# Two tiles of a feed-forward projection without Strassen, token blocks made once, and a new order of the products

## The chip, the cores and the metric

The kernel runs on one core of a Trainium2 chip. A core has five engines with queues of their own: TensorE (PE, matmuls into PSUM), VectorE (DVE), ScalarE (ACT), GpSimd (POOL) and SyncE (SP, which issues DMAs here). The metric is the device time of one execution in microseconds, lower is better.

## The reference, cut to what matters

One layer of a transformer trunk for 512 latent and 128 context tokens of 1024 features. The change concerns its second half, from the output projection of the attention part to the first feed-forward projection:

```python
x += gate1 * (merged @ w_out)                       # 640 x 1024
h = rms_norm(x, norm2_w) * (1 + scale2) + shift2
a, up = split(h @ w_ffn_in)                         # 1024 -> 2 x 2816
a = dwconv3(a)                                      # along the tokens, latent and context apart
x += gate2 * ((silu(a) * up) @ w_ffn_out)           # 2816 -> 1024
y = rms_norm(x, final_norm_w)
```

## The kernel before, in words

Every float32 matrix is split into a high and a low part, `hi` and `lo` (a cast on ScalarE and a subtraction, usually on VectorE), and each product of 128 x 128 weights with 320 tokens is made of hi*hi, hi*lo and lo*hi. The 640 tokens are two halves of 320 (`HALF`), the 1024 features two halves of four blocks. So one block product, called a product here, is 4 x 3 = 12 matmuls.

The first feed-forward projection runs over 22 tiles of 128 columns. In a tile the column block of `a` (raw weights `raw_fa`) and that of `up` (`raw_fu`) against the two token halves would be eight products. The kernel uses Strassen's scheme in Winograd's form with seven: `product(i, p)` for p = 1, 2, 5, 6, 3, 7, 4. It needs sums of weight blocks (`sums`, four operations of 128 x 512 on POOL per tile) and differences of token blocks. Products 1, 2, 5 and 3 read `h2` (whose tiles print as `mg`), products 6, 7 and 4 read `hx`, the blocks that are sums. Two accumulators, `pfNA` and `pfNC` of tile N, are one PSUM pair, and `pb` takes product 2. Behind them `copy`, `add2`, `add3` and `add7` bring the parts together (`av`, `c`), `conv` makes one ScalarE and four VectorE operations into `cv`, `silu` and the multiplications (`glu2`, `glu1`) end in the split tile `g` (`glo` its low part).

The tiles are in three groups of 8, 7 and 7 (`GROUPS`). After a group the second projection (`out2_steps`) takes the group's tiles as its sum; weights come block by block through `fetch`. In group 0 it shares its time with the making of the second gate (`gate2`, matmuls `pb_g`). Within a group `cycle(i)` writes down the work of tile i, the rest of tile j = i - 1 and the weights of n = i + 1. `start` is the hand-written order of the first tiles. The order of each engine's instructions is the order in which the code is written (`Pin`), for PE, VectorE, ScalarE and POOL alike.

Ahead of `start`, `out_steps(t)` makes the output projection of token tile t (PSUM `pso`), the gated sum (`y`, `x`), the norm, and `modulate(t)` transposes the result (`pt`) and modulates it. For tokens of the second half `modulate` also makes, per token tile, the differences `e` and their splits, on VectorE and POOL. For the last token tile the first products of tiles 0, 1 and 2 are put ahead of its transposes.

## Time and profile before

| | |
|---|---|
| median of 3 runs (lowest to highest) | 1103.39 us (1103.24 to 1106.56) |
| the profiled execution | 1106.75 us |
| its span, first to last instruction | 1104.7 us |
| mean granted TensorE clock | 0.98 |
| busy: PE, DVE, ACT, POOL | 1046.0, 858.2, 549.2, 346.8 us |

The profiled execution is 0.3% above the median and 2 us longer than its span. Busy shares are means over stages that differ: the attention part, the 70 us around the start of the feed-forward part, and the long run of cycles after it.

### The profile page before, as it was taken

The numbers are of one execution on the slowest core, as the hardware profiler recorded it, in microseconds if no ns is written. First come the engines' busy times: TensorE is split into PE (matmuls) and PEld (weight loads), VectorE is DVE, ScalarE is ACT, GpSimd is POOL, SyncE is SP. The second block draws the span as 40 slices with busy tenths as digits, with TensorE's granted clock in tenths as the row PEclk, the third lists the DMA queues.
The fourth block names the chain that finished last, engine by engine and source line by source line (L and its number), as shares of the span: only waits on it lengthen the run. The fifth ranks groups of instructions, "written<-read, shape, count | busy, mean of one in ns | idle before, by whom it ended". The sixth has DMA issues, their size and how long they took to land. (4 is left out here: it accounts for less than half of the span.)

```text
span 1104.7 us, 16747 instructions
## 1 busy us (share of the span) xinstructions
PE 1046.0 (95%) x6535; PEld 974.3 (88%) x6535; DVE 858.2 (78%) x1197; ACT 549.2 (50%) x913; POOL 346.8 (31%) x279
## 2 busy tenths in 40 slices
PE   6988999999999999999999978899999999999997
PEld 4788899999999999999998768899789998899986
DVE  5968988988887577776763599899769984599847
ACT  8636667667665552222343554555344552255524
POOL 3544324323222630000000196344175320444202
PEclk9898999999999999999999989899999999999999
DMA  9830212112112135554562021324442232222412
GB/s 313 231 94 27 84 32 65 47 38 65 41 42 58 49 88 170 153 155 140 164 194 112 1 58 39 96 77 134 126 122 77 77 118 63 69 77 77 133 39 96
DMA packets 128481, 106.11 MB, mean 96 GB/s; under 512 B 4173, under 2 KB 110205, under 8 KB 128402
## 3 DMA queue, kind: packets, MB, share of 16 engines
q1 hardware_dynamic: 126450, 101.93, 30.6%
q0 software_dynamic: 1232, 1.80, 0.8%
q8 instruction: 51, 0.84, 0.3%
q10 hardware_dynamic: 720, 1.31, 0.3%
q14 instruction: 28, 0.23, 0.1%
HBM read 101.36 MB, written 3.67 MB: 95 GB/s over the span
## 5 line engine op out<-in xcount | busy, mean ns | idle before, releaser
L157 PE MATMUL ps_g<-hT,whi_g 128*128 128x320 f32 x512 | 96.7, 311 | 0.0
L150 DVE SCALAR_TENSOR_TENSOR cv<-av,vcol,cv 128x511 f32<-128x511 f32 (+1 forms) x84 | 85.5, 1038 | 7.7 <-ACT cv L150 6.4
L150 POOL TENSOR_TENSOR s<-raw_fu 128x512 f32<-128x512 f32 x20 | 30.2, 1509 | 165.4 <-DMA raw_fu<-in_w_ffn_in_dram 91.8
L157 PEld LDWEIGHTS ps_g<-hT,whi_g 128*128 128x128 f32 x512 | 80.2, 188 | 2.0 <-issue 1.5
L150 ACT CAST whi_f<-s 128x1024 fp32r<-128x1024 f32 x42 | 44.1, 1049 | 65.6 <-POOL s L150 54.5
L689 ACT ACTIVATE p<-s,nm 128x640 f32<-128x640 f32 (+1 forms) x80 | 56.5, 708 | 40.0 <-DVE nm L687 39.4
L157 PE MATMUL psv<-whi_v,hT 128*128 128x256 f32 x320 | 66.3, 287 | 0.0
L687 DVE TENSOR_REDUCE nm<-s 128x1 f32<-128x640 f32 (+1 forms) x80 | 56.6, 710 | 12.4 <-PE s L157 11.0
L150 DVE TENSOR_TENSOR wlo_f<-s,whi_f 128x1024 fp32r<-128x1024 f32 x42 | 54.7, 1302 | 8.8 <-ACT whi_f L150 8.8
L157 PE MATMUL ps_g<-hT,wlo_g 128*128 128x320 f32 x256 | 58.3, 309 | 0.0
L242 DVE SCALAR_TENSOR_TENSOR acc_g<-raw_g,silu,acc_g 128x512 f32<-128x512 f32 x48 | 40.9, 886 | 20.4 <-DMA raw_g<-in_w_ada_dram 18.9
L157 PE MATMUL s<-ks,qd 128*128 128x320 f32 x144 | 44.2, 318 | 10.3 <-DVE ks L598 7.1
L157 PEld LDWEIGHTS psv<-whi_v,hT 128*128 128x128 f32 x320 | 53.5, 193 | 0.3 <-ACT whi_v L126 0.3
L157 PE MATMUL psyb<-on,whi_pb 128*128 128x320 f32 x256 | 48.0, 309 | 0.0
L127 DVE TENSOR_TENSOR wlo_fo<-raw_fo,whi_fo 128x1024 fp32r<-128x1024 f32 (+1 forms) x24 | 28.3, 1179 | 23.6 <-ACT whi_fo L126 23.5
L157 PE MATMUL psv<-wlo_v,hT 128*128 128x256 f32 x160 | 45.6, 285 | 0.9 <-DVE wlo_v L127 0.9
L126 ACT CAST whi_fo<-raw_fo 128x1024 fp32r<-128x1024 f32 (+1 forms) x24 | 23.5, 978 | 39.6 <-PE acc101C L157 15.6
L157 PE MATMUL s<-ks,ql 128*128 128x320 f32 x144 | 43.0, 309 | 0.0
L157 PEld LDWEIGHTS ps_g<-hT,wlo_g 128*128 128x128 f32 x256 | 42.8, 188 | 0.0
L157 PE MATMUL psk<-hT,whi_k 128*128 128x320 f32 x224 | 42.6, 312 | 0.0
L157 PEld LDWEIGHTS psyb<-on,whi_pb 128*128 128x128 f32 x256 | 40.3, 188 | 0.5
L157 PE MATMUL pb<-mg,whi_f 128*128 128x320 f32 x176 | 40.6, 318 | 0.0
(1009 smaller groups left out, 3450.1 us busy)
## 6 DMA issues: line engine op xcount, KB each, us to landing
raw_fa<-in_w_ffn_in_dram SPq DMA_DIRECT2D x22, 512.0 KB, 4.5
raw_fu<-in_w_ffn_in_dram SPq DMA_DIRECT2D x20, 512.0 KB, 4.0
raw_fo<-in_w_ffn_out_dram SPq DMA_DIRECT2D x20, 512.0 KB, 4.8
raw_g<-in_w_in_dram SPq DMA_DIRECT2D x16, 512.0 KB, 4.6
raw_g<-in_w_ada_dram SPq DMA_DIRECT2D x16, 512.0 KB, 3.7
araw_sh<-in_w_ada_dram SPq DMA_DIRECT2D x8, 512.0 KB, 8.2
araw_sc<-in_w_ada_dram SPq DMA_DIRECT2D x8, 512.0 KB, 9.1
raw_v<-in_w_in_dram SPq DMA_DIRECT2D x8, 512.0 KB, 6.3
```

The lines of the kernel that those rows point to most:

```text
L126: nc.scalar.copy(hi[:, :n], rv)
L127: eng.tensor_tensor(lo[:, :n], rv, f(hi[:, :n]), ALU.subtract)
L150: pin(getattr(self.eng, op)(*args, **kw))
L157: pin(nc.tensor.matmul(out, s, m, start=start, stop=stop, skip_group_check=more))
L242: nc.vector.scalar_tensor_tensor(acc[:, c, :], raw[:, ki, :], w, acc[:, c, :], ALU.mult, ALU.add)
L687: nc.vector.tensor_reduce(nm[:, i:i + 1], s, AX.XY, ALU.max, negate=True)
L689: nc.scalar.activation(p.rearrange("p (b n) -> p b n", b=s.shape[1]), s, AF.Exp, bias=nm[:, i:i + 1], accum_out=z[:, i:i + 1])
```

## The change

Tiles 0 and 1 (`DIRECT`) are made as ordinary products, eight each: 1, 2, then Q, D, E, F, G and H, which read raw weights and `h2` alone. They need neither `sums` nor `hx`. Their parts are joined by `addD` and `glu_direct`.

`modulate` keeps all tokens in one tile, `hall`, and makes only the difference that `h2` itself needs, in place. The blocks of `hx` are made once, for all 320 tokens, by `blocks` and `block_lo` on VectorE behind the last token tile. POOL no longer takes part in this, nor in the low parts of the first weights. In the last token tile four products stand ahead of the transposes, and a high and a low part of tile 1's weights are put between its steps.

In a cycle the products go 1, 2, the last tile's 7, 5, 6, 3, the last tile's 4, where 4 stood ahead of 3; the splits follow in the order in which the products use them, each later than before. In group 0 `glo` follows four tiles late, so `cv` has three buffers.

The first weights of `out2_steps` are fetched in the last cycle of a group, `prepare` of the next group's first tile is in two parts, and the steps of the second gate go to the (block, token tile) pairs of `GATE2`. The operations of the gate's sums and of the fetched weights' splits now keep the written order too (not shown). Of `start` only the new lines are shown.

```diff
+    DIRECT = 2
+    R, S, W2, PS, PB, PD, AV, C22, CVS, GT = {}, {}, {}, {}, {}, {}, {}, {}, {}, {}
...
-        src = {1: lambda: R[i, 0], 2: lambda: S[i, 0], 3: lambda: S[i, 1], 4: lambda: R[i, 1][:, 4:, :]}[n]()
-        if n < 4:
+        src = {1: lambda: R[i, 0], 2: lambda: S[i, 0], 3: lambda: S[i, 1], 4: lambda: R[i, 1][:, 4:, :],
+               5: lambda: R[i, 1]}[n]()
+        if n != 4:
             w = [wpool.tile([P, KD, P], F32R, tag=t, name=f"{t}_f{n}_{i}") for t in ("whi", "wlo")]
...
+            for k0, ps in zip((0, 4), {1: ((1, "E"), (2, "F")), 2: ((5,), (6,)), 3: ((3,), (7,)),
+                                       5: (("Q", "G"), ("D", "H"))}[n]):
+                for p in ps:
+                    W2[i, p] = [x[:, k0:k0 + 4, :] for x in w]
...
+            elif p == "D":
+                PD[i] = psF.tile([P, 512], F32, tag="F", name=f"pd{i}")[:, :HALF]
+            out = {1: pa, 6: pa, 7: pa, 4: pa, 5: pc, 3: pc, 2: PB.get(i), "Q": pc, "D": PD.get(i),
+                   "E": pa, "F": pa, "G": pc, "H": pc}[p]
...
+    def addD(i):
+        dve.tensor_tensor(C22[i], C22[i], PD.pop(i), ALU.add)
+    def glu_direct(i):
+        dve.tensor_tensor(CVS[i][:, :HALF], CVS[i][:, :HALF], C22.pop(i), ALU.mult)
+        dve.tensor_tensor(CVS[i][:, HALF:], CVS[i][:, HALF:], PS.pop(i)[1][:, :HALF], ALU.mult)
...
+        cv = CVS[i] = pools["ffn"].tile([P, TOK], F32, tag="cv", name=f"cv{i}", bufs=3)
...
+        ghi(i)
+    def ghi(i):
...
+            if before:
+                before()
             half(1)
+            if between:
+                between()
...
-            h32 = h1[:, :, ts] if t < 2 else wo.tile([P, KD, P], F32, tag="h32", name=f"h32_{t}", bufs=1)
...
+            yield
+            c0, c1 = max(t * P, HALF), (t + 1) * P
+            if t * P < HALF:
+                cs = slice(t * P, min(c1, HALF))
+                split_to(h2[0][:, :, cs], h2[1][:, :, cs], hall[:, :, cs])
+            if c0 >= c1:
                 return
...
-            b12, b22 = h32[:, :4, lead:], h32[:, 4:, lead:]
-            e = wo.tile([P, 16, P], F32, tag="e", name=f"e{t}", bufs=1)
-            e1, e2, e3, e4 = (e[:, 4 * i:4 * i + 4, :n] for i in range(4))
-            dve.tensor_tensor(e1, b12, h1[:, :4, cs], ALU.subtract)
-            dve.tensor_tensor(e2, b22, e1, ALU.subtract)
-            split_to(h2[0][:, :4, c2], h2[1][:, :4, c2], e1)
+            c2, b12 = slice(c0, c1), hall[:, :4, c0:c1]
+            dve.tensor_tensor(b12, b12, hall[:, :4, c0 - HALF:c1 - HALF], ALU.subtract)
+            split_to(h2[0][:, :4, c2], h2[1][:, :4, c2], b12)
             yield
-            split_to(hx[0][:, :4, cs], hx[1][:, :4, cs], e2)
-            split_to(h2[0][:, 4:, c2], h2[1][:, 4:, c2], b22)
-            yield
-            pool.tensor_tensor(e3, b22, b12, ALU.subtract)
-            pool.tensor_tensor(e4, h1[:, 4:, cs], e2, ALU.subtract)
-            yield
-            split_to(hx[0][:, 4:, cs], hx[1][:, 4:, cs], e[:, 8:, :n], dve if t == NT - 1 else pool)
+            split_to(h2[0][:, 4:, c2], h2[1][:, 4:, c2], hall[:, 4:, c2])
+        def blocks(n):
+            b11, b21, e1, b22 = (hall[:, k:k + 4, c:c + HALF] for c in (0, HALF) for k in (0, 4))
+            e = EB[n] = spare[1][:, 2 * n:2 * n + 2, :].rearrange("p j n -> p (j n)").rearrange("p (k n) -> p k n", n=HALF)
+            x, y = ((b22, e1), (b21, EB.get(0)), (EB.get(0), b11))[n]
+            dve.tensor_tensor(e, x, y, ALU.subtract)
+            act.copy(hx[0][:, KB[n], :], e)
+        EB, KB = {}, (slice(0, 4), slice(8, 12), slice(4, 8))
+        def block_lo(n):
+            dve.tensor_tensor(hx[1][:, KB[n], :], EB[n], f(hx[0][:, KB[n], :]), ALU.subtract)
...
+            last = t == NT - 1
+            if last:
                 load(0, 0)
+                load(0, 1)
                 load(1, 0)
-                load(2, 0)
-            for n in out_steps(t, True):
+            for n in out_steps(t, True, last and (lambda: hi(1, 1)), last and (lambda: lo(1, 1))):
                 if n == (11, 9, 9)[t - 2]:
                     rest = modulate(t - 1)
-                    next(rest, None)
+                    next(rest)
                     next(rest, None)
                 elif n == (15, 13, 10)[t - 2]:
                     each(rest)
-                if t == NT - 1 and n in (1, 3):
-                    hi(n // 2, 1)
-                elif t == NT - 1 and n in (2, 4):
-                    lo(n // 4, 1, pool)
-                elif t == NT - 1 and n == 13:
-                    hi(2, 1)
+                if last and n == 1:
+                    hilo(0, 1)
+                elif last and n == 4:
+                    hilo(0, 5)
+                    load(1, 1)
         spare = [res.tile([P, 8, TOK], F32, tag=f"r{i}", name=f"spare{i}") for i in range(2)]
...
-        load(0, 1, room(0, 0))
-        load(1, 1, room(1, 0))
-        lo(2, 1, pool)
-        product(0, 1, 2)
-        product(1, 1)
-        copy1(0, spare[0][:, 7, :])
+        product(0, 1, 2, "Q", "D")
+        copy1(0, spare[0][:, 0, :])
         act.activation(warm2, eps, AF.Silu)
         add2(0)
-        sums(0, 0, room(0, 2))
         rest = modulate(NT - 1)
         next(rest)
-        product(2, 1)
-        product(1, 2)
-        hilo(0, 2)
-        sums(0, 1, room(1, 2))
+        hilo(1, 5)
+        copy5(0, spare[0][:, 2, :HALF])
+        addD(0)
+        load(2, 0)
+        load(2, 1)
+        product(1, 1, 2)
+        copy1(1, spare[0][:, 1, :])
         next(rest)
-        hilo(0, 3)
-        product(2, 2)
-        product(0, 5)
-        copy5(0, spare[1][:, 7, :HALF])
-        product(0, 6)
+        add2(1)
         each(rest)
+        product(1, "Q", "D")
+        copy5(1, spare[0][:, 3, :HALF])
+        addD(1)
+        for n in range(3):
+            blocks(n)
+        block_lo(0)
+        product(0, "E", "F")
+        copy6(0)
+        hilo(2, 1)
     actx.close()
...
-    def prepare(i):
-        load(i, 0)
-        load(i, 1)
+    def prepare(i, part):
+        if part == 0:
+            load(i, 0)
+            load(i, 1)
+            hilo(i, 1)
+            return
         sums(i, 0)
-        hilo(i, 1)
+        hilo(i, 2)
         sums(i, 1)
-        hilo(i, 2)
         hilo(i, 4)
         load(i + 1, 0)
-        hilo(i, 3)
         load(i + 1, 1)
-    def cycle(i, first, end):
...
+    def cycle(i, first, end, after):
         j, n = (i - 1 if i > first else None), (i + 1 if i < end else None)
...
         product(i, 1, 2)
         do(j, lambda j: product(j, 7))
         do(j, add3)
-        do(j - 1 if j is not None and j > first else None, glo)
+        copy1(i)
+        if i == DIRECT + 1:
+            lo(i, 3)
+        elif i == first:
+            hilo(i, 3)
+        if i - 4 >= GROUPS[0][0] and first == DIRECT:
+            glo(i - 4)
+        elif j is not None and j > first and first != DIRECT:
+            glo(j - 1)
         do(j, conv)
-        copy1(i)
         do(n, sums, 0)
-        do(n, hi, 2)
         add2(i)
         do(j, add7)
-        do(n, lo, 2)
+        product(i, 5)
+        copy5(i)
+        if n is None:
+            next(after)
+        do(n, hi, 1)
+        do(n, lo, 1)
         do(j, silu)
         do(j, glu2)
-        do(n, hi, 1)
-        product(i, 5)
+        do(n, hi, 2)
         do(n, sums, 1)
-        copy5(i)
-        do(n, lo, 1)
-        do(n, hi, 4)
-        do(n, lo, 4)
+        do(n, lo, 2)
+        if i == DIRECT + 1:
+            lo(i, 4)
         product(i, 6)
         if i + 2 <= end:
             load(i + 2, 0)
         copy6(i)
         do(n, hi, 3)
+        product(i, 3)
+        do(n, lo, 3)
         do(j, lambda j: product(j, 4))
+        do(n, hi, 4)
         do(j, glu1)
-        do(n, lo, 3)
-        product(i, 3)
+        do(n, lo, 4)
         if i + 2 <= end:
             load(i + 2, 1)
...
     def start():
...
+        sums(2, 0)
+        load(3, 0)
         conv(0)
+        product(0, "G", "H")
+        hilo(2, 2)
+        sums(2, 1)
+        load(3, 1)
+        product(1, "E", "F")
+        copy6(1)
         silu(0)
+        hi(2, 3)
+        glu_direct(0)
+        lo(2, 3)
+        product(1, "G", "H")
+        product(2, 1, 2)
         copy1(2)
+        sums(3, 0)
+        hi(3, 1)
         add2(2)
+        lo(3, 1)
+        hi(2, 4)
+        block_lo(2)
+        product(2, 5)
+        copy5(2)
+        conv(1)
+        hi(3, 2)
+        lo(2, 4)
+        lo(3, 2)
+        silu(1)
+        sums(3, 1)
+        product(2, 6)
+        copy6(2)
+        load(4, 0)
+        block_lo(1)
+        hi(3, 4)
+        hi(3, 3)
+        glu_direct(1)
         gates_of(0)
+        ghi(0)
+        ghi(1)
         product(2, 3)
         load(4, 1)
+    GATE2 = ((0, 2), (1, 0), (1, 2), (2, 0), (3, 2), (3, 4), (4, 0), (4, 2), (5, 0), (5, 2), (7, 1), (7, 3))
...
+        out2 = out2_steps(g, hook)
+        for i in range(DIRECT + 1 if g == 0 else first, end + 1):
+            cycle(i, DIRECT if g == 0 else first, end, out2)
+        product(end, 7)
         add3(end)
-        glo(end - 1)
+        glo(end - 3 if g == 0 else end - 1)
         conv(end)
+        add7(end)
         silu(end)
-        def hook(hf, ends, i):
-            if g == 0 and (ends and i in (0, 2)):
-                next(later, None)
-        out2 = out2_steps(g, hook)
-        next(out2)
-        product(end, 7)
-        add7(end)
         glu2(end)
         next(out2)
         product(end, 4)
         glu1(end)
-        glo(end)
-        while True:
-            for _ in range(2 if g == 0 else 0):
-                next(later, None)
-            if next(out2, out2) is out2:
-                break
+        for i in range(end - 2 if g == 0 else end, end + 1):
+            glo(i)
+        for _ in out2:
```

On PE, around the transposes of the last token tile (`pt`, reading its normalised rows `y`), before the change (`pf1A` is tile 1's first product, `pf2A` tile 2's):

```order
L157 MATMUL pf1A_6683<-mg0_4510,whi_f1_1_6562 128x320
L157 MATMUL pf1A_6683<-mg1_4511,whi_f1_1_6562 128x320
L157 MATMUL pf1A_6683<-mg0_4510,wlo_f1_1_6563 128x320
L160 MATMUL pt2_40_6703<-ident_73,y4_6543 128x128 x4
L160 MATMUL pt2_41_6712<-ident_73,y4_6543 128x128 x4
L157 MATMUL pf2A_6726<-mg0_4510,whi_f1_2_6632 128x320
L157 MATMUL pf2A_6726<-mg1_4511,whi_f1_2_6632 128x320
L157 MATMUL pf2A_6726<-mg0_4510,wlo_f1_2_6633 128x320
```

and after it (`pd` is product D of tile 0):

```order
L157 MATMUL pd0_6673<-mg0_4510,whi_f5_0_6554 128x320
L157 MATMUL pd0_6673<-mg1_4511,whi_f5_0_6554 128x320
L157 MATMUL pd0_6673<-mg0_4510,wlo_f5_0_6555 128x320
L160 MATMUL pt2_40_6689<-ident_73,y4_6533 128x128 x4
L160 MATMUL pt2_41_6698<-ident_73,y4_6533 128x128 x4
L157 MATMUL pf1A_6717<-mg0_4510,whi_f1_1_6619 128x320
L157 MATMUL pf1A_6717<-mg1_4511,whi_f1_1_6619 128x320
L157 MATMUL pf1A_6717<-mg0_4510,wlo_f1_1_6620 128x320
```

The transposes had three products ahead of them, 1 and 2 of tile 0 and 1 of tile 1; now it is 1, 2, Q and D of tile 0, and what follows them needs tile 1 where it needed tile 2.

On VectorE, from the last modulation ahead of the last token tile's second half to its norm, before the change (`h` and `e` are the modulated rows and differences of token tile 3, `mg` and `hx` low parts, `y` and `x` the gated sum of the last token tile):

```order
L150 TENSOR_SCALAR h32_3_6588<-pt2_30_6589,sc2_96,sh2_97 128x128 x4
L150 TENSOR_TENSOR e3_6607<-h32_3_6588,h1_6163 128x512
L150 TENSOR_TENSOR e3_6607<-h32_3_6588,e3_6607 128x512
L150 TENSOR_TENSOR mg1_4511<-e3_6607,mg0_4510 128x4x128
L150 TENSOR_TENSOR hx1_6152<-e3_6607,hx0_6151 128x4x128
L150 TENSOR_TENSOR mg1_4511<-h32_3_6588,mg0_4510 128x4x128
L150 TENSOR_TENSOR y4_6543<-pso4C_6542,acc_g11_5920 128x512
L150 TENSOR_TENSOR x2_4_6150<-x2_4_6150,y4_6543 128x512
L150 TENSOR_SCALAR ss2_4_6544<-ss2_4_6544 128x1
L150 RECIPROCAL rstd_n2_4_6645<-rstd_n2_4_6645 128x1
L150 TENSOR_SCALAR y4_6543<-x2_4_6150,rstd_n2_4_6645 128x512
```

and after it (`hall` holds the modulated rows):

```order
L150 TENSOR_SCALAR hall_6163<-pt2_30_6578,sc2_96,sh2_97 128x128 x4
L150 TENSOR_TENSOR hall_6163<-hall_6163 128x4x128
L150 TENSOR_TENSOR mg1_4511<-hall_6163,mg0_4510 128x4x128 x2
L150 TENSOR_TENSOR y4_6533<-pso4C_6532,acc_g11_5920 128x512
L150 TENSOR_TENSOR x2_4_6150<-x2_4_6150,y4_6533 128x512
L150 TENSOR_TENSOR wlo_f1_1_6620<-raw_fa1_6529,whi_f1_1_6619 128x1024
L150 TENSOR_SCALAR ss2_4_6534<-ss2_4_6534 128x1
L150 RECIPROCAL rstd_n2_4_6627<-rstd_n2_4_6627 128x1
L150 TENSOR_SCALAR y4_6533<-x2_4_6150,rstd_n2_4_6627 128x512
```

Two differences and a low part of `hx` stood ahead of the second `y` and no longer do; a low part of tile 1's weights now stands behind its `x`.

On ScalarE, around the copies of tile 3's products 1 and 5 (`av` from `pf3A`, `c` from `pf3C`), before the change (`cv` is the convolution, `g` the gated product, `whi_f` and `uh` high parts of weights):

```order
L150 CAST uh_2_7033<-raw_fu2_6817 128x512
L150 CAST uh_3_7037<-raw_fu3_6933 128x512
L150 CAST whi_f3_3_7043<-s1_3_7010 128x1024
L150 ACTIVATE cv2_7102<-av2_6904,vcol_88 128x640
L150 COPY av3_7108<-pf3A_7061 128x320
L150 CAST whi_f2_4_7113<-s0_4_7110 128x1024
L150 ACTIVATE cv2_7102<-cv2_7102 128x640
L150 CAST whi_f1_4_7121<-raw_fa4_7041 128x1024
L150 COPY c22_3_7139<-pf3C_7062 128x320
L150 CAST uh_4_7142<-raw_fu4_7059 128x512
L150 COPY av3_7108<-pf3A_7061 128x320
```

and after it:

```order
L150 ACTIVATE cv1_6977<-cv1_6977 128x640
L150 COPY av2_6949<-pf2A_6922 128x320
L150 CAST uh_3_7008<-raw_fu3_6864 128x512
L150 CAST whi_f3_3_7011<-s1_3_6989 128x1024
L150 CAST g00_7016<-cv0_6827 128x640
L150 CAST g00_7016<-cv1_6977 128x640
L150 COPY av3_7074<-pf3A_7034 128x320
L150 ACTIVATE cv2_7077<-av2_6949,vcol_88 128x640
L150 COPY c22_3_7100<-pf3C_7035 128x320
L150 CAST whi_f1_4_7102<-raw_fa4_7005 128x1024
L150 ACTIVATE cv2_7077<-cv2_7077 128x640
```

Before, casts of weights stood between the copies; now two casts of gated tiles, `g` from the `cv` of tiles 0 and 1, and two of weights stand ahead of tile 3's first copy, and the convolution of tile 2 behind it.

## Rows read from the trace of the kernel before

**Rows 1.** The page: busy time of each engine, share of the span, instructions.
```profile
PE 1046.0 (95%) x6535; PEld 974.3 (88%) x6535; DVE 858.2 (78%) x1197; ACT 549.2 (50%) x913; POOL 346.8 (31%) x279
```
**Rows 2.** What PE waited for after 600 us: total, times, longest.
```profile
PE pt L160 <- DVE y L150: 7.8, 2, 6.9
PE pf3A L157 <- DVE wlo_f L150: 4.1, 1, 4.1
PE pf0C L157 <- DVE wlo_f L150: 2.4, 2, 1.7
PE pf2A L157 <- DVE c L150: 2.1, 1, 2.1
PE pf9A L157 <- DVE wlo_f L150: 1.8, 1, 1.8
PE pf0A L157 <- DVE spare L150: 0.9, 1, 0.9
PE pf9A L157 <- DVE c L150: 0.9, 1, 0.9
...
PE pb_g L157 <- ACT g L280: 0.7, 1, 0.7
```
**Rows 3.** PE's timeline: start, duration, what, and idle time before with its releaser.
```profile
633.93 1.09 PE L160 MATMUL pt<-ident,y 128*128 128x128 f32 x8 [0.89 <-DVE y L150]
634.78 2.33 PE L157 MATMUL pso4C<-woA,mg 128*128 128x512 f32 x9
...
639.03 0.45 PE L157 MATMUL pf0A<-mg,whi_f 128*128 128x320 f32 x2
...
651.33 1.94 PE L160 MATMUL pt<-ident,y 128*128 128x128 f32 x8 [6.90 <-DVE y L150]
...
706.17 0.56 PE L157 MATMUL pf2A<-hx,uh 128*128 128x320 f32 x2 [2.10 <-DVE c L150]
...
709.77 0.45 PE L157 MATMUL pf4A<-mg,whi_f 128*128 128x320 f32 x2
```
**Rows 4.** Windows: length, busy time per engine (instructions), granted clock, DMA share, GB/s.
```profile
648.00:660.00 12.00, 8.67 (x44) 8.70 (x45) 9.76 (x13) 8.70 (x16) 11.84 (x9) 0.63 0.15 45
...
684.00:696.00 12.00, 7.92 (x46) 7.65 (x45) 9.76 (x9) 5.00 (x9) 5.81 (x4) 0.80 0.12 34
696.00:708.00 12.00, 9.90 (x61) 9.63 (x61) 11.44 (x14) 5.78 (x9) 5.46 (x4) 0.92 0.36 100
708.00:720.00 12.00, 11.98 (x83) 11.72 (x82) 11.67 (x14) 6.91 (x10) 5.52 (x4) 1.00 0.32 87
...
872.20:884.40 12.20, 12.18 (x84) 11.92 (x83) 11.87 (x15) 6.60 (x10) 5.52 (x4) 1.00 0.32 87
```
**Rows 5.** VectorE's timeline at token tiles 2 and 3 and the last.
```profile
617.41 0.68 DVE L150 TENSOR_TENSOR y<-pso2C,acc_g 128x512 f32<-128x512 f32 x1
...
620.14 0.48 DVE L150 TENSOR_SCALAR y<-x,rstd_n 128x512 f32<-128x512 f32 x1
...
638.36 1.57 DVE L150 TENSOR_TENSOR e<-h,h 128x512 f32<-128x512 f32 x1
...
644.98 0.68 DVE L150 TENSOR_TENSOR mg<-h,mg 128x512 fp32r<-128x512 f32 x1
645.58 0.68 DVE L150 TENSOR_TENSOR y<-pso4C,acc_g 128x512 f32<-128x512 f32 x1
```
**Rows 6.** POOL's timeline, the first of a tile's four sums.
```profile
684.56 1.31 POOL L150 TENSOR_TENSOR s<-raw_fu 128x512 f32<-128x512 f32 x1 [4.00 <-DMA raw_fu<-in_w_ffn_in_dram]
```
**Rows 7.** VectorE's timeline: a split and a convolution, beside POOL and alone.
```profile
658.88 2.31 DVE L150 TENSOR_TENSOR wlo_f<-spare,whi_f 128x1024 fp32r<-128x1024 f32 x1
...
668.94 1.21 DVE L150 TENSOR_TENSOR wlo_f<-s,whi_f 128x1024 fp32r<-128x1024 f32 x1
...
673.58 2.18 DVE L150 SCALAR_TENSOR_TENSOR cv<-spare,vcol,cv 128x511 f32<-128x511 f32 x4 [1.05 <-ACT cv L150]
...
684.63 6.04 DVE L150 SCALAR_TENSOR_TENSOR cv<-av,vcol,cv 128x511 f32<-128x511 f32 x4
```

More of the change, by code (lines that the diff above doesn't have):

```diff
@@ L237, in ada_acc @@
                     if c and part:
[L238 to L240 removed]
+                        y = space.tile([P, 512], F32, tag=part, name=f"part_{name}{hf}{u}{ki}")
+                        act.activation(y, raw[:, ki, :], AF.Copy, scale=w)
+                        pool.tensor_tensor(acc[:, c, :], acc[:, c, :], y, ALU.add)
                         continue
[L242 removed]
+                    (dve if part else nc.vector).scalar_tensor_tensor(acc[:, c, :], raw[:, ki, :], w, acc[:, c, :],
+                                                                      ALU.mult, ALU.add)
             yield acc
@@ L1073, in product @@
                 for n, (w, x) in enumerate(((wh, ah), (wh, al), (wl, ah))):
-                    mm(out, w[:, k, :], x[:, k, :], p in (1, 2, 5) and k + n == 0, k == 3 and n == 2, p in (6, 7, 4, 3))
+                    mm(out, w[:, k, :], x[:, k, :], p in (1, 2, 5, "Q", "D") and k + n == 0, k == 3 and n == 2,
+                       p not in (1, 2, 5, "Q", "D"))
     def copy1(i, dst=None):
@@ L1137, in trunk_kernel, with out_steps @@
         Y2 = {}
-        def out_steps(t, by_half=False):
+        def out_steps(t, by_half=False, before=None, between=None):
             ts = slice(t * P, (t + 1) * P)
@@ L1329, in fetch @@
             if n == len(todo):
-                if not final:
-                    prepare(first + size)
                 return
@@ L1335, in fetch @@
             for u, m in blk:
-                wh, wl = wcols(w_fo, hf * 512, 512, first + u, m, f"fo{g}{hf}{u}")
+                wh, wl = wcols(w_fo, hf * 512, 512, first + u, m, f"fo{g}{hf}{u}", *(() if final else (dve, act)))
                 for j in range(m):
                     W[n][u + j] = wh[:, j, :], wl[:, j, :]
+            if n == len(todo) - 1 and not final:
+                prepare(first + size, 0)
         if final:
@@ L1367, in out2_steps @@
                             j == 0, j == size - 1)
-                hook(hf, ends, i)
+                hook(n, i)
+                if not final and n == len(todo) - 1 and i == (0 if g else 3):
+                    prepare(first + size, 1)
             if not ends:
@@ L1507, in trunk_kernel, with hook @@
             gates_of(g)
-        for i in range(3 if g == 0 else first, end + 1):
-            cycle(i, first, end)
-        add3(end)
-        glo(end - 1)
-        conv(end)
-        silu(end)
-        def hook(hf, ends, i):
-            if g == 0 and (ends and i in (0, 2)):
+        def hook(n, i):
+            if g == 0 and (n, i) in GATE2:
                 next(later, None)
         out2 = out2_steps(g, hook)
-        next(out2)
+        for i in range(DIRECT + 1 if g == 0 else first, end + 1):
+            cycle(i, DIRECT if g == 0 else first, end, out2)
         product(end, 7)
+        add3(end)
+        glo(end - 3 if g == 0 else end - 1)
+        conv(end)
         add7(end)
+        silu(end)
         glu2(end)
```

93 lines of the change are left out of this document (13 added, 80 removed).

## Prediction

> **What bounds the kernel now.** The page comes first: TensorE (PE) is busy for 1046.0 us, 95% of the span, VectorE (DVE) for 858.2 us [rows 1]. With such a share there are two ways to be faster: fewer matmuls, or less of the remaining idle time and of the time at the lower clock. The change has more matmuls, so the second place to look is the list of what PE waited for [rows 2]. One wait stands out: 6.9 us for the tile `y`, the last token tile's normalised half. Behind it come 4.1 for `wlo_f`, 2.1 for `c`, 2.4 in two pieces for `wlo_f`, .9 for `spare`. In time, the first of them ends at 651.33 and the last at 706.17 [rows 3], so all of them lie between the end of the attention part's output projection and the first steady cycle, that of tile 4, which starts at 709.77. Third, I read that stretch by its windows [rows 4]: PE is busy 8.67, 7.92 and 9.90 us of 12, and the granted clock falls to 0.63 in the window behind the 6.90 us of idling and to 0.80 in that of the 4.08 us. In a steady cycle, by contrast, PE has 12.18 of 12.20 us, full clock, and 84 matmuls: 12.2/84 = .145 us each, 1.745 us for a product of 12.
>
> What the stretch loses is then one subtraction. Its first product starts at 639.03, tile 4 at 709.77 [rows 3]: 70.7 us. In it lie 26 products and eight transposes. Eight transposes took .85 us from start to next start for tile 3 (633.93 to 634.78 [rows 3]), so at full clock 26 x 1.745 + .85 = 46.2 us would do, and 24.5 are lost. The waits are 6.9 + 4.1 + 2.4 + 2.1 + .9 = 16.4 [rows 2]; the other 8.1 are mostly the lower clock of the windows at 0.63, 0.80 and 0.92 [rows 4], and some .15 us behind each wait until the pipeline is full.
>
> Why `y` is late stands in VectorE's own timeline [rows 5]. From 638.36 it makes the token blocks of tile 3, five operations until 645.58, and only then starts on `y`, although PE was through with that input when it began the next product at 639.03 [rows 3]. The first of them takes 1.57 us and the last, when GpSimd (POOL) has paused, .68, for the same 512 columns; POOL is working on blocks of the same tile. From the start of `y` to the transposes (651.33 [rows 3]) it is 5.75 us, where the same chain of tile 2 took 3.2 (617.41 to 620.62).
>
> **The change, part by part.**
>
> *More matmuls.* Tiles 0 and 1 take 8 products instead of 7: 24 matmuls x .145 = 3.5 us, all on PE. Their weight sums go (eight POOL operations, 1.31 us each when undisturbed [rows 6]), and with them what PE waited for at `pf0C`: their splits need raw weights only, which SyncE now loads during the last token tile.
>
> *The end of the attention part.* Of VectorE's five block operations per half tile three are left ahead of `y`, and POOL has nothing to do, so they should take .68 each: free at about 639.5 instead of 645.58. `y` starts there: the wait of .89 us for tile 3's `y` [rows 3] goes too, for the same reason, so that the projection ends and the first product starts at 639.03 - .89 = 638.1. Then come .7 + .7, the new low part of tile 1's split, 1.21 [rows 7], between the add and the norm, and the rest of tile 2's chain, 1.8: `y` is ready near 644.5 to 645.3. PE now has four products before the transposes, until 638.1 + 4 x 1.745 = 645.1. So of 6.9 us about .2 stay. Bounds: nothing, or, if VectorE's operations stayed at 1.8, another 3.4. I add .35 for the second group of transposes, whose bank is freed only by an add behind it on VectorE, and .3 for the split of tile 1's other weights, which stands behind the modulation. These two are estimates, parts of one operation of .68 [rows 5] and of one of 1.21 [rows 7].
>
> *From there to tile 4.* The products that need no blocks (tiles 0 and 1) come first, the blocks are made meanwhile, in three subtractions of 1280 columns. No such operation is in the trace. By 1.21 for 1024 columns it is 1.5; in company of POOL, by 2.31 [rows 7], 2.6 to 2.9. In the order of instructions VectorE has 44 steps from 645.1 to the last product of tile 2, which needs `c` of tile 2; with each at its undisturbed duration I add up 33.4 us (an estimate: 6.5 for the last token tile's blocks and the adds among them, 9 for three blocks and three low parts of 1280 columns, 7.3 for six splits of 1024, 6.5 for three convolutions at 2.18 [rows 7], the rest small adds). PE has 28 products and the transposes, so would start that product, the 28th, at 638.1 + 27 x 1.745 + .85 = 686.1, 41 us later. VectorE fits, at 81%. In two places it does not, locally. (a) The copy of tile 3's first product on ScalarE now stands behind two casts that wait for tile 1's gated product on VectorE; behind it PE's third-from-last product of the stretch waits, and the conv of tile 2 on ScalarE. I put 1.2 us; bounds 0 and 2.1, the wait for `c` of before. (b) That product of tile 2 needs an add behind its convolution's four operations on VectorE. They take 2.18 alone and 6.04 beside POOL [rows 7], and POOL will be on tile 4's sums. 3.7 of 3.9 us of stretching would show, as PE has nothing else to do; bounds 1.5 and 5. (c) A wait of that size lowers the clock: behind the 4.1 us the window has 0.80, behind the 2.1 us [rows 3] it is 1.00 again. I put 1.0 us, half of what 2 us of matmuls become; bounds 0 and 2.3. With .15 of refilling for each of the three larger waits, new losses are .2 + .35 + .3 + 1.2 + 3.7 + 1.0 + .4 = 7.15.
>
> So the stretch changes by -24.5 - .9 + 3.5 + 7.15 = -14.75 us, and tile 4 should start at 695.0.
>
> *The steady cycles.* The products and their number are the same; only 3 and the last one of the tile before change places, as do the splits. PE is busy 12.18 of 12.20 [rows 4] and cannot gain. VectorE is at 11.87 of 12.20 and its operations are the same ones, so I take 0, with a bound of +.3 (idle time that is left to VectorE) either way for each of 17 cycles, mostly not in the same direction.
>
> *Between the groups.* The first weights of the second projection are fetched a cycle earlier, and the next group's first tile is prepared in two parts. Before, that start cost 1.8 for `wlo_f` and .9 for `c` at tile 9 [rows 2]; both go. The gate's steps are put at other blocks: .7 for `pb_g` [rows 2] goes and comes back elsewhere, since the gate's broadcast needs its accumulation, a cast and a split (the split 1.2) in order; I put 2 us, bounds 0 and 4. Sum -1.8 - .9 - .7 + 2 = -1.4.
>
> Together -14.75 - 1.4 = -16.2 us. The profiled execution took 1106.75 us, 2 us more than its span, and would become 1090.6; the median of the runs is 1103.39, 0.3% lower, which becomes **1087**.
>
> **A rule against it.** The row says that an operation of 1024 columns with both inputs in SBUF takes 2.31 us instead of 1.21 when POOL is working, 1.1 us more [rows 7]. The Trainium skill, "SBUF — State Buffer", section "SBUF: two separate sides", says that the shared port pair is an exclusive lock: of a VectorE operation with two SBUF inputs and a GpSimd operation that reads SBUF, whoever starts second waits out the other. By that each of the ten POOL operations of the stretch could hold up VectorE by its whole 1.3 us, 13 us in all rather than the 11 of ten times 1.1; by the rule the third case would be 1097, by the rows it is the 1095 below. The trace agrees with the rule as far as the 1.1 us go; a whole blocked operation stands in no row here.
>
> **The rivals.**
>
> *VectorE keeps up everywhere.* For it: 33.4 of 41 us, and the blocks are off POOL. Against: (a) and (b) are in the order of instructions. Without new losses: -24.5 - .9 + 3.5 = -21.9, and -1.8 - .9 - .7 = -3.4 for the later waits: 1103.4 - 25.3 = 1078.
>
> *VectorE becomes the bound of the start.* POOL has ten sums between 659 and the start of tile 4; if each costs VectorE its 1.1 us, 33.4 becomes 44.4, which is 3.4 over the 41, before (a) and (b). PE then waits in four or five places, and two windows at 0.8 or below come back as before, 2 to 4 us of work at half clock. That adds 6 to 10 to the forecast: 1093 to 1097, say 1095.
>
> *The new order of the cycle is longer than the old one: slower.* VectorE has .33 us to spare in 12.20 [rows 4]. The low part of split 1 now waits behind the copy of the fifth product, and the last gated product stands behind a product that comes 1.74 later than before; if that chain closes the loop from one tile to the next, every cycle grows. 16.2 us are used up at .95 us per cycle in 17 cycles; with 1.2 the time is 1087 + 20.4 = 1107. Against it: the last product has 1.74 us more room for its own input, and no operation is added.
>
> *No change.* The transposes wait as before, because `y` hangs on something that I did not see (ScalarE's square, the split put ahead of it): -16.2 + 6.9 + 4 for the clock (half of the 8.1) leaves -5.3; with a cycle longer by .3, 17 x .3 = 5.1, nothing is left, 1103.
>
> **How the numbers follow.** Forecast (1082 to 1092, the bounds of (a), (b) and the gate) .50, VectorE keeping up .20, VectorE the bound .18, longer cycles .08, no change .04. A measurement of this kernel cannot tell less than about 0.3%, 3.3 us, from nothing: faster is below 1100. The first three are faster, .88; the last gives .04 for no change; the longer cycles .08 for slower. The range takes in the second and third case and leaves out the last two: 1077 to 1098.
>
> **What would show it.** Right: the wait for `y` at the transposes is under 1 us and no window between 638 and 660 is below 0.9; tile 4's first product starts 13 to 16 us earlier, at 693 to 697; the largest waits left are for `c` of tile 2 and behind the copy of tile 3; cycles stay at 12.2. A start of tile 4 near 689 is the second case, one past 701 with VectorE over 11.5 of 12 us is the third, and cycles of over 12.5 us the fourth. Wrong it would be, above all, if the cycles are longer, since that counts 17 times, or if the gate's waits in the second projection of group 0 are much over 4 us.

## The result, and the profile after

The changed kernel takes 1092.6 us (median of 4 runs, 1091.4 to 1094.0); the kernel before, on the same chip, 1103.3. The ratio is 0.9896 (95% interval 0.9873 to 0.9919): 1% or 10.7 us faster, where 16.2 were forecast. The time lies in the range, 5.6 us above the point.

The profiled executions differ by 15.1 us of span, 1089.6 against 1104.7. That is too much, and PE's timeline shows by how much: the first matmul of token tile 3's output projection, ahead of which the change moves nothing, starts at 613.97 in the kernel before,

```profile
613.97 0.40 PE L157 MATMUL pso3A<-woA,mg 128*128 128x512 f32 x1
```

and after the change at 609.66:

```profile
609.66 0.40 PE L157 MATMUL pso3A<-woA,mg 128*128 128x512 f32 x1
```

So 4.3 us belong to the part in front. From this matmul to the end of the span it is 490.7 us before and 479.9 after: -10.8, as the medians say. This distance, called the path below, carries the comparisons, since the front part differs from execution to execution. A kernel has one path, that of its profiled execution. Over all kernels below, the median less the path lies between 612.4 and 614.5, so the two agree to some 2 us, and a difference of path smaller than that decides little.

In PE's timeline after the change, the four products run into the last transposes without a gap (8 transposes, no releaser named), where [rows 3] had 6.90 us; what waits is listed behind them, and tile 4 starts at 689.45 (4.3 us of its lead belong to the front part, so it is 693.8 on the clock of the kernel before):

```profile
640.54 1.40 PE L160 MATMUL pt<-ident,y 128*128 128x128 f32 x8
641.70 0.54 PE L157 MATMUL pf1A<-mg,whi_f 128*128 128x320 f32 x2
...
676.76 0.41 PE L157 MATMUL pf2A<-hx,whi_f 128*128 128x320 f32 x1 [1.37 <-ACT av L150]
...
687.59 0.56 PE L157 MATMUL pf2A<-hx,uh 128*128 128x320 f32 x2 [2.94 <-DVE c L150]
...
689.45 0.45 PE L157 MATMUL pf4A<-mg,whi_f 128*128 128x320 f32 x2
...
828.59 0.56 PE L157 MATMUL pf8A<-hx,uh 128*128 128x320 f32 x2 [1.78 <-DVE c L150]
```

The list of PE's waits after 600 us (total, times, longest), against [rows 2]:

```profile
PE pf2A L157 <- DVE c L150: 2.9, 1, 2.9
PE pb_g L157 <- DVE bl_g L250: 2.4, 2, 1.4
PE pf8A L157 <- DVE c L150: 1.8, 1, 1.8
PE pf15A L157 <- DVE c L150: 1.5, 1, 1.5
PE pf2A L157 <- ACT av L150: 1.4, 1, 1.4
PE pf3A L157 <- DVE c L150: 1.3, 1, 1.3
PE pf19A L157 <- DVE c L150: 0.6, 1, 0.6
...
PE pf4A L157 <- DVE c L150: 0.5, 1, 0.5
```

The old wait for `y` is gone, and so are those for splits `wlo_f` at the start; two of .5 us are left at tiles 8 and 9 (not shown). More than half of what is left, 9.4 of 15.9 us, is one kind: product 4 of a tile waits for `c`. And the windows (columns as in [rows 4]) show full clock throughout the start, and one drop, where tile 8's product 4 had waited:

```profile
636.00:648.00 12.00, 11.73 (x81) 11.22 (x80) 8.19 (x16) 8.35 (x18) 0.00 (x0) 1.00 0.22 62
648.00:660.00 12.00, 12.00 (x85) 12.00 (x84) 10.46 (x11) 6.92 (x8) 5.33 (x3) 1.00 0.09 28
...
684.00:696.00 12.00, 9.06 (x63) 8.80 (x62) 10.97 (x15) 5.45 (x8) 4.04 (x4) 1.00 0.39 112
826.00:831.34 5.34, 3.56 (x19) 3.30 (x18) 5.30 (x8) 2.98 (x5) 1.59 (x2) 0.81 0.06 14
```

On the path, tile 4 starts 16.0 us earlier than before; from there to tile 8 the kernel loses 3.6 of it, from tile 8 to tile 15 .2, and from tile 15 to the end 1.4.

### The profile page after: what moved, and what is told of

It is laid out like the page before. It is cut to its first block, busy times and chain, and to the rows that moved or that the text cites. A ratio compares the mean times of both kernels' runs of the same rounds, so it can differ in the third digit from the quotient of the medians.

```text
span 1089.6 us, 16713 instructions
## 1 busy us (share of the span) xinstructions
PE 1038.0 (95%) x6559; PEld 967.0 (89%) x6559; DVE 851.6 (78%) x1193; ACT 543.5 (50%) x906; POOL 320.8 (29%) x256
## 4 chain that ended last, share of the span: by engine, by line
PE 54%; DVE 28%; ACT 8%; issue 7%; POOL 1%; DMA 1%; SPq 0%; ACTq 0%; DVEq 0%; POOLq 0%
PE ps_g L157 10%; DVE cv L150 7%; PE psyb L157 5%; PE psk L157 3%; PE psu L157 3%; PE psya L157 3%; DVE wlo_f L150 3%; PE s L157 2%; PE acc L157 2%; PE po L157 2%; DVE nm L688 2%; PE psv L157 2%; PE psq L157 2%; ACT cv L150 1%; PE pat L160 1%
## 5 line engine op out<-in xcount | busy, mean ns | idle before, releaser
L150 POOL TENSOR_TENSOR s<-raw_fu 128x512 f32<-128x512 f32 x20 | 33.3, 1666 | 309.1 <-DVE spare L150 155.7
L150 DVE SCALAR_TENSOR_TENSOR cv<-av,vcol,cv 128x511 f32<-128x511 f32 (+1 forms) x80 | 88.8, 1130 | 12.1 <-ACT cv L150 10.8
L150 DVE TENSOR_TENSOR wlo_f<-s,whi_f 128x1024 fp32r<-128x1024 f32 x40 | 51.0, 1298 | 4.7 <-ACT whi_f L150 4.6
L157 PE MATMUL s<-ks,qd 128*128 128x320 f32 x144 | 44.2, 318 | 10.7 <-DVE ks L599 7.1
L150 ACT CAST whi_f<-s 128x1024 fp32r<-128x1024 f32 x40 | 41.8, 1044 | 12.0 <-POOL s L150 11.9
L697 ACT ACTIVATE p<-p,z 128x640 f32<-128x640 f32 (+1 forms) x40 | 29.7, 744 | 20.0 <-DVE z L696 19.8
L157 PEld LDWEIGHTS s<-ks,qd 128*128 128x128 f32 x144 | 27.6, 192 | 13.4 <-POOL ry_q L562 6.8
L698 DVE SCALAR_TENSOR_TENSOR p<-p,z,p 128x640 f32<-128x640 f32 (+1 forms) x40 | 35.0, 878 | 5.4 <-ACT p L697 5.1
L150 POOL TENSOR_TENSOR acc_g<-acc_g,part_g 128x512 f32<-128x512 f32 x16 | 27.9, 1743 | 37.7 <-ACT part_g L150 36.8
```

The costliest lines, as they stand in the source:

```text
L150: pin(getattr(self.eng, op)(*args, **kw))
L157: pin(nc.tensor.matmul(out, s, m, start=start, stop=stop, skip_group_check=more))
L697: nc.scalar.activation(p, p, AF.Copy, scale=z[:, 1:2])
L698: nc.vector.scalar_tensor_tensor(A[h, t], A[h, t], z[:, 0:1], p, ALU.mult, ALU.add)
```

## The experiments

Theory 1: VectorE, held up by POOL in its operations with two SBUF inputs, is late, and TensorE waits for `c` again and again. Theory 2: the new order of the cycle costs the missing 5 us. Theory 3: ScalarE's queue. Theory 4: it is only the place of one add on VectorE. All kernels are the changed one with the edit shown, but for the one that says otherwise. The last column counts from the same matmul to the first product of tile 4.

| run | median us | ratio to before, interval | path us | start to tile 4 |
|---|---|---|---|---|
| before | 1103 to 1105 | | 490.7 | 95.8 |
| changed | 1092.6 | 0.9896, 0.9873 to 0.9919 | 479.9 | 79.8 |
| old_cycle | 1097.4 | 0.9925, 0.9899 to 0.9951 | 484.8 | 83.6 |
| no_sums | 1075.0 | 0.9732, 0.9707 to 0.9757 | 460.6 | 74.3 |
| act_order | 1090.8 | 0.9881, 0.9854 to 0.9908 | 478.3 | 80.6 |
| pool_company | 1097.3 | 0.9927, 0.9901 to 0.9954 | 482.7 | 83.9 |
| three_products | 1095.6 | 0.9919, 0.9894 to 0.9945 | | |
| add7_mid | 1085.6 | 0.9818, 0.9798 to 0.9838 | 471.5 | 77.2 |
| conv2 | 1084.6 | 0.9809, 0.9786 to 0.9832 | 470.6 | 76.5 |
| conv2_mid_act | 1082.3 | 0.9793, 0.9771 to 0.9815 | 468.9 | 76.3 |
| dve_sums | 1082.5 | 0.9795, 0.9771 to 0.9819 | 468.2 | 77.0 |
| before_dve_sums | 1100.6 | 0.9969, 0.9955 to 0.9983 | 487.8 | 94.5 |
| best_a | 1079.7 | 0.9768, 0.9738 to 0.9799 | 465.1 | 75.3 |
| best_b | 1076.4 | 0.9748, 0.9726 to 0.9770 | 463.8 | 75.0 |

The path is one profiled execution's, the median that of all runs. Of three_products no profile is used.

**old_cycle.** `cycle` with the old places of products 3 and 4 and of the splits.

> The changed kernel, with the products and splits of a cycle in the order of the kernel before (product 4 of the tile before ahead of product 3; the start and the steps between the groups as changed). Theory 1, VectorE's backlog: VectorE comes out of the start late, beside POOL it has no time to spare in a cycle, and so TensorE waits for `c` ahead of product 4 in cycle after cycle. Then the old order, where product 4 comes 1.74 us earlier, makes each of these waits longer, by up to 1.74 us at tiles 2 to 5, 8 and 15: 1094 to 1101 us. Theory 2, the new order of the cycle is itself what costs: these waits go with it, 1088 to 1090 us.

1097.4, path +4.9, 3.8 of it ahead of tile 4. Theory 2 falls: the old order is not faster. The waits for `c` from VectorE grew at tiles 2, 4 and 5 as theory 1 has it, but at tiles 3, 8 and 16 others took their place (`av` and `c` from ScalarE, a split), and in all they fell from 9.4 to 7.2 us:

```profile
PE pf2A L157 <- DVE c L150: 3.6, 1, 3.6
PE pf16A L157 <- DVE wlo_f L150: 2.4, 1, 2.4
PE pf8C L157 <- ACT c L150: 2.1, 1, 2.1
...
PE pf5A L157 <- DVE c L150: 1.5, 1, 1.5
PE pf4A L157 <- DVE c L150: 1.4, 1, 1.4
```

All waits of the path together are 16.9 us against 15.9. What is longer is the time at the lower clock: 0.72 in the window below, where the changed kernel has 1.00, and 0.57 in the 4 us from 820 and in those from 960. So most of the 4.9 is clock.

```profile
684.00:696.00 12.00, 8.44 (x41) 8.18 (x40) 11.30 (x14) 5.60 (x8) 4.75 (x4) 0.72 0.28 79
```

**no_sums.** It leaves the sums out, so it does not compute the layer; only its time is of use.

```diff
         ra, ru = R[i, 0], R[i, 1]
+        if i > 2:
+            S[i, b] = (ru, ra)[b]
+            return
```

> The changed kernel without POOL's sums of weight blocks from tile 3 on: the raw weight blocks are split in their place, so every other engine has its operations of the same sizes in the same order. Theory 1 (VectorE is late because its operations with two SBUF inputs stand still beside POOL's): a convolution's four operations take 2.2 us everywhere, the waits for `c` of 9.2 us in all go, and the one of 1.37 us for `av`: 1082 to 1085 us. Theory 2 (the order of the cycle): the waits stay, 1091 to 1093 us.

1075.0, path -19.3, more than expected: no wait for `c`, `av` or a split `wlo_f` is left in the list, and full clock at tile 8. A steady cycle (12.26 us of PE) had 11.92 us of VectorE,

```profile
856.51:868.77 12.26, 12.26 (x86) 12.26 (x85) 11.92 (x15) 6.57 (x10) 6.49 (x4) 1.00 0.30 85
```

and without sums 9.07, with the same operations:

```profile
844.41:856.67 12.26, 12.26 (x86) 12.26 (x85) 9.07 (x15) 6.82 (x10) 0.00 (x0) 1.00 0.31 87
```

So POOL's four operations cost VectorE 2.85 us a cycle. This is theory 1's mechanism, .71 us for each POOL operation. The Trainium skill ("SBUF — State Buffer", section "SBUF: two separate sides") calls the port that VectorE and GpSimd share an exclusive lock. The trace agrees with that in kind: VectorE's operations are longer beside POOL's; but the price is not a POOL operation's whole 1.6 us (6.49 for four in the first window).

**act_order.** `silu(1)` behind `copy6(2)`, `ghi(0)` and `ghi(1)` behind `conv(2)`.

> The changed kernel with two changes on ScalarE alone: the silu of tile 1 behind the copy of tile 2's sixth product, and the casts of the gated tiles 0 and 1 behind tile 3's first copy and tile 2's convolution. Theory 3, ScalarE's queue is what is left at the start: the waits of 1.37 and .33 us go and stay gone, 1.7 us faster, 1091 us. Theory 1: they go, but the wait for `c` of tile 2 grows by as much, since VectorE sets when that is ready: 0 to .5 us faster, 1092 to 1092.6 us.

The path is 1.6 shorter, as theory 3 has it, but not where: tile 4 starts .8 later (a wait of 1.5 us for `c` from ScalarE is new), and the stretch from tile 4 to tile 8 is 2.2 shorter. The intervals overlap with the changed kernel's; it decides little.

**pool_company.** Ahead of `half(1)` of the last token tile:

```diff
+                for _ in range(10):
+                    pool.tensor_tensor(junk, x2[4][:, :512], x2[4][:, :512], ALU.add)
```

> The changed kernel with ten POOL additions of 128x512 into an unused tile beside the last token tile's second half, as much as POOL did there before the change (nothing reads them). If POOL's company made `y` late before: VectorE's operations there take 1 us more each, `y` is 5 to 6 us later, TensorE waits some 5 us at the transposes, the granted clock falls behind it, and the time is 1097 to 1101 us. If it was the number of VectorE's own block operations: a wait under 1.5 us and 1092 to 1094 us.

Path +2.8, tile 4 4.1 later. VectorE's timeline before the change, beside what POOL did then:

```profile
640.03 1.60 DVE L150 TENSOR_TENSOR e<-h,e 128x512 f32<-128x512 f32 x1
...
643.27 1.78 DVE L150 TENSOR_TENSOR hx<-e,hx 128x512 fp32r<-128x512 f32 x1
...
646.29 2.26 DVE L150 TENSOR_TENSOR x<-x,y 128x512 f32<-128x512 f32 x1
```

after the change, and then with the company:

```profile
633.71 0.69 DVE L150 TENSOR_TENSOR hall<-hall 128x512 f32<-128x512 f32 x1
635.23 1.29 DVE L150 TENSOR_TENSOR mg<-hall,mg 128x512 fp32r<-128x512 f32 x2 [0.82 <-ACT mg L150]
...
637.76 1.22 DVE L150 TENSOR_TENSOR wlo_f<-raw_fa,whi_f 128x1024 fp32r<-128x1024 f32 x1
...
639.67 0.48 DVE L150 TENSOR_SCALAR y<-x,rstd_n 128x512 f32<-128x512 f32 x1
```

```profile
638.53 1.48 DVE L150 TENSOR_TENSOR hall<-hall 128x512 f32<-128x512 f32 x1
640.70 2.21 DVE L150 TENSOR_TENSOR mg<-hall,mg 128x512 fp32r<-128x512 f32 x2 [0.69 <-ACT mg L150]
...
644.28 2.06 DVE L150 TENSOR_TENSOR wlo_f<-raw_fa,whi_f 128x1024 fp32r<-128x1024 f32 x1
...
647.02 0.50 DVE L150 TENSOR_SCALAR y<-x,rstd_n 128x512 f32<-128x512 f32 x1
```

From the first row of either to its last it is 5.96 us alone and 8.49 in company, 2.5 more, and PE waited for `y`:

```profile
647.67 0.63 PE L160 MATMUL pt<-ident,y 128*128 128x128 f32 x4 [2.14 <-DVE y L150]
```

That lies between the two expectations. Company alone brings back 2.1 of the 6.9 us; how the rest divides is not shown. VectorE has two operations less there, but the 1.60 and 1.78 us that they took were stretched too; `x` took 2.26 beside a POOL operation of 1024 columns and .81 beside these of 512; and the fourth product covers 1.75. Most of the rest of the 4.1 is clock: behind the wait of 3.0 us for `c` of tile 2 it is 0.63 in the 4 us from 694, where the changed kernel, behind 2.94 at the same place, stays at 1.00.

**three_products.** Product D of tile 0 behind the transposes.

> The changed kernel with product D of tile 0 behind the last token tile's transposes instead of ahead of them, so that three products are ahead as in the kernel before. In the changed kernel's profile `y` was finished at 640.16 and the four products ran to 640.54. With three, TensorE is there 1.75 us earlier and waits 1.4 us. If the filler counts: 1.4 us more at the transposes, and 1 to 1.6 us more in all: 1093.6 to 1094.2 us. Rival: VectorE's later lateness swallows it and tile 4 starts no later than before: 1092.6 us.

1095.6 is 3 us above the changed kernel, in the expected direction, but the intervals of the ratios overlap and no profile is used: open.

**add7_mid.**

```diff
         for s0, s1 in ((0, LAT), (LAT, TOK)):
+            if s0 and between:
+                between()
             dve.scalar_tensor_tensor(cv[:, s0 + 1:s1], av[:, s0:s1 - 1], w[0], cv[:, s0 + 1:s1], ALU.mult, ALU.add)
...
+            conv(j, lambda: (add2(i), add7(j)))
```

> The changed kernel with VectorE's two adds that follow a convolution (of product 2 and of product 7, which gives `c`) put between its second and third operation. Theory 1, capacity: VectorE has no time to spare, so the lateness moves on to its next operations, the low parts of weights and the gated products, and TensorE waits there instead: 1 to 4 us faster, 1088 to 1091 us. Theory 4, only the place: `c` is 2.5 to 3 us earlier, ahead of product 4 everywhere but at tile 2, the waits of 5 us and a window at the lower clock go: 5 to 8 us faster, 1084 to 1087 us.

1085.6, path -8.5: theory 4. The waits for `c` are gone but for .3; at tile 4 alone a split is late in their place, and the clock is 0.69 in the 4 us from 692.

```profile
PE pf4A L157 <- DVE wlo_f L150: 1.8, 1, 1.8
PE pf2A L157 <- ACT av L150: 1.4, 1, 1.4
...
PE pf2A L157 <- DVE c L150: 0.3, 1, 0.3
```

So VectorE does all its work in a cycle's time. What was late was one add of .47 us, because it stood behind a convolution that takes 5.07 us beside POOL at tile 2 and 5.75 in the steady cycle above (2.18 alone, [rows 7]). The place is not all of it: the path gains 8.5 us of the 19.3 that go without sums.

**conv2.** Two operations of 639 columns for four; ScalarE mends the columns at the border (`neg` holds the negated weights, `av` is kept for it).

```diff
-        for s0, s1 in ((0, LAT), (LAT, TOK)):
...
+        dve.scalar_tensor_tensor(cv[:, 1:], av[:, :TOK - 1], w[0], cv[:, 1:], ALU.mult, ALU.add)
+        dve.scalar_tensor_tensor(cv[:, :TOK - 1], av[:, 1:], w[2], cv[:, :TOK - 1], ALU.mult, ALU.add)
...
     def silu(i):
...
+        for j, d, s_ in ((0, LAT, LAT - 1), (2, LAT - 1, LAT)):
+            act.activation(cv[:, d:d + 1], av[:, s_:s_ + 1], AF.Identity, bias=cv[:, d:d + 1],
+                           scale=neg[:, j // 2, i:i + 1])
```

> The changed kernel with a convolution of two VectorE operations of 639 columns for four of 511 and 127 (the two columns at the border of the streams are mended by two one-column operations on ScalarE ahead of the silu). Theory 1, each VectorE operation with two SBUF inputs that meets POOL stands still once, by about a us: two operations less save 1.3 us or more of VectorE's time per cycle, the waits for `c` shrink to under 1 us each from tile 3 on, 1084 to 1088 us. Rival, each POOL operation holds VectorE up once, whatever it is doing: the same four POOL operations cost the same, only at other places, and .35 us per cycle are saved: 1089 to 1092 us.

1084.6, path -9.3, theory 1's time. VectorE's groups by shape (busy, mean ns) from 690 to 1000 us in the changed kernel:

```profile
L150 DVE SCALAR_TENSOR_TENSOR cv<-av,vcol,cv 128x511 f32<-128x511 f32 x32 | 40.5, 1265 | 10.2 <-ACT cv L150 9.6
L150 DVE SCALAR_TENSOR_TENSOR cv<-av,vcol,cv 128x127 f32<-128x127 f32 x31 | 33.4, 1076 | 0.5
...
L150 DVE TENSOR_TENSOR cv<-cv,c 128x320 f32<-128x320 f32 x15 | 7.2, 481 | 0.9 <-ACT cv L150 0.9
```

and with two operations:

```profile
L150 DVE SCALAR_TENSOR_TENSOR cv<-av,vcol,cv 128x639 f32<-128x639 f32 x32 | 45.3, 1415 | 9.6 <-ACT cv L150 9.0
...
L150 DVE TENSOR_TENSOR cv<-cv,c 128x320 f32<-128x320 f32 x16 | 19.6, 1227 | 2.6 <-ACT cv L150 2.3
```

A convolution takes 2.8 us instead of 4.7, but the multiplication by `c` behind it now meets POOL: .48 became 1.23. The rival is right in that: POOL's stretch moves on to whatever comes next. VectorE's busy time says so too: in the four cycles of tiles 10 to 13 it is 47.1 us against 48.3, .3 a cycle as the rival has it, not 1.3. So theory 1's time came by the rival's mechanism. That it is again the earlier `c` that pays fits the waits for it, 1.7 us in all against 9.4 (1.2 of them at tile 3).

**conv2_mid_act, dve_sums.** The first is conv2, add7_mid and act_order in one; the second:

```diff
+        e = dve if i > 2 else pool
         if b == 0:
-            pool.tensor_tensor(s[:, :4, :], ru[:, :4, :], ru[:, 4:, :], ALU.add)
+            e.tensor_tensor(s[:, :4, :], ru[:, :4, :], ru[:, 4:, :], ALU.add)
...
```

> The changed kernel with the two-operation convolution, the two adds between its operations, and ScalarE's silu and casts moved as in the run of ScalarE's order. If VectorE's lateness is all that TensorE still waits for in the cycles, every wait for `c` and `av` goes but the one at tile 2: 1079 to 1083 us. If they overlap in what they save: 1084 to 1088 us.

> The changed kernel with the sums of weight blocks from tile 3 on made by VectorE instead of POOL. Without sums a cycle had 9.07 us of VectorE's time and with POOL beside it 11.9, so each of POOL's four operations cost VectorE .71 us; made by VectorE itself they are four of .68. Theory 1: VectorE has 11.8 us of 12.2 per cycle, as many as before, but none of it depends on when POOL starts: 1089 to 1095 us. Rival: VectorE cannot take them, since the sums now stand in line with the splits that wait for them, and becomes the bound with cycles over 12.6 us: 1097 to 1104 us.

1082.3 is in the first expectation's bounds, though the path shows overlap: 11.1 us for parts of 9.3, 8.5 and 1.6. The other is a surprise: VectorE makes the sums itself and the kernel is 10 us faster than with POOL's help, better than either theory. Its window of a steady cycle has the 11.8 us foreseen:

```profile
850.11:862.37 12.26, 12.26 (x86) 12.26 (x85) 11.89 (x19) 7.09 (x11) 0.00 (x0) 1.00 0.30 87
```

As much VectorE time as with POOL. But the convolution is short again, by the same groups from 690 to 1000 us:

```profile
L150 DVE SCALAR_TENSOR_TENSOR cv<-av,vcol,cv 128x511 f32<-128x511 f32 x33 | 24.8, 751 | 9.9 <-ACT cv L150 9.4
...
L150 DVE SCALAR_TENSOR_TENSOR cv<-av,vcol,cv 128x127 f32<-128x127 f32 x32 | 11.2, 349 | 0.6
```

So the add that gives `c` starts 8.1 us after the first product of this cycle, where it was 9.8 in the changed kernel's, although two of the four sums stand between the convolution and it (the other two behind it). The waits for `c` fall from 9.4 to 3.5 us in all.

**before_dve_sums.** The same edit in the kernel before the change.

> The kernel before the change, with the sums of weight blocks from tile 3 on made by VectorE instead of POOL. If POOL's sums cost it as they cost the changed kernel (11.7 us there): waits at tiles 2, 3, 5, 7 and 9 shrink, 1093 to 1098 us. Rival: the old order of the cycle, with product 4 ahead of 3 and the first split last, leaves the sums no room in VectorE's line, and TensorE waits for splits: 1103 to 1112 us.

1100.6, between the two: path -2.9. The waits for `y` stay at 7.8, the one for `wlo_f` at tile 3 is 1.3 instead of 4.1, and new ones for `c` from ScalarE come at tiles 8 and 15. The edit gave 11.7 in the changed kernel; which part of the change makes the room for it was not tried.

**best_a, best_b.** dve_sums, add7_mid and act_order in one; with conv2 added.

> The changed kernel with three of the edits together: sums from tile 3 on made by VectorE, the two adds in the middle of the convolution, and ScalarE's silu and casts moved. Alone, counted from the same start of the projection, they gave 11.7, 8.4 and 1.6 us. If they end the same waits: 1080 to 1083 us. If they add up to all that waits and clock cost in the cycles (19 us without any sums): 1074 to 1079 us.

> As the run before, with the convolution of two VectorE operations added. With POOL idle in the cycles the two operations less save only .35 us of VectorE's time per cycle, which has .4 us to spare, and ScalarE's two small operations lengthen the way to the silu by .5 us: no different from the run before, within 1.5 us either way. If VectorE's capacity is still the limit at tiles 3 to 9 and 20: 2 to 4 us faster.

1079.7 and 1076.4: both beat both kernels, by 2.3% and 2.5% against the one before. best_a is .3 us below its first case, that the edits end the same waits. Which of the two is better, the intervals do not tell (path 1.3 apart). In best_b the path is 3.2 us longer than without any sums; the longest waits left after 600 us:

```profile
PE pb_g L157 <- DVE bl_g L251: 1.2, 2, 0.8
PE pf9A L157 <- DVE wlo_f L150: 0.8, 1, 0.8
```

## Why the prediction was right in its direction and 5 us too fast

*What bounds the kernel, and the start:* right. The loss between the projection and tile 4 went: 16.0 us on the path, 14.75 forecast. The start of tile 4 at 689.45 looks like the sign of the second case, but less the front part's 4.3 us it is 693.8, inside the forecast's 693 to 697. The wait for `y` went fully, by POOL's absence, fewer operations and the fourth product (pool_company shows the first). How the 16.0 divides among the tiles made directly, the blocks made once and the fourth product no run shows. One reading of the rows was wrong there: from 635.13 to 641.08 POOL worked on low parts of the first weights, not on blocks; the change took both away. Of the new losses, (b) was forecast at 3.7 and is 2.94, at the place named; (a) at 1.2 and is 1.37 + .33, but the larger part at another place: product 7 of tile 2, whose copy stands behind tile 1's silu, behind tile 1's stretched convolution. (c), the clock, was 1.0 and is nothing: 1.00 in the window of the 2.94 us. That is in part luck, since behind 3.0 us at the same place pool_company has 0.63.

*The steady cycles, "I take 0":* this step failed. Waits for `c` go on at tiles 3, 4 and 5 (1.26, .54, .32 us), and at tiles 8, 15, 16, 17 and 19; behind the start of tile 4 they sum to 6.5 us. Before they were 2.1, the .9 at tile 9 [rows 2] and

```profile
PE pf5A L157 <- DVE c L150: 0.8, 1, 0.8
...
PE pf7A L157 <- DVE c L150: 0.4, 1, 0.4
```

From tile 4 to tile 8, with the gate, the kernel lost 3.6 us where the sum had +1.3 (2 for the gate less .7). The forecast gave the last product 1.74 us more room for its input, and nearly all of that went: over nine steady cycles (tiles 10 to 14 and 17 to 20) the add that gives `c` starts 9.7 us after the cycle's first product, where it was 8.1, because in the new order the convolution begins .9 us later and is stretched more, 5.2 us against 4.4; with the old order put back it is 7.7. I read 11.87 of 12.20 us on VectorE as "no gain, no loss" and did not ask which of its operations would meet POOL. That the lateness is POOL's, no_sums shows; that the place of the add decides over the waits for `c`, add7_mid shows (9.4 us become .3). That an operation late once catches up only slowly is argued, not shown.

*Between the groups, "both go":* wrong too. In place of the 1.8 for `wlo_f` at tile 9 come two waits of .5 for splits of tiles 8 and 9, a wait of 1.78 for `c` of tile 8 came, with the clock at 0.81 behind it, and at tile 15 a new one of 1.48. From tile 8 on the path is 1.6 us longer than before, where -2.7 was in the sum. These 4.3 us and the 2.3 more between tiles 4 and 8, less the 1.25 by which the start was better, are the difference between 16.2 and 10.8. The gate's 2 us were 2.4, and .3 for its other half.

*The rivals.* VectorE as bound of the start did not come at the start; its mechanism, POOL's company, came in the cycles, and the time of 1092.6 lies between the forecast's 1087 and that case's 1095. The longer cycle did not come: a steady cycle is 12.26 us where it was 12.20, and with the old order the path is 4.9 longer, not shorter.

## What to carry to other kernels

When an engine is near full in a steady loop, look at which of its operations somebody waits for and put those first; its busy share alone says little: two kernels with 11.9 us of VectorE per cycle differ by 11.7 us. Work that is given to GpSimd to relieve VectorE has to be priced with what it takes from VectorE: here .71 us for an operation that VectorE does in .68; in the kernel before the same edit gave only 2.9 us of path. And compare profiled executions from a matmul behind the last unchanged part, not from the start of the span.
